# Half of a modulation's columns summed on VectorE, and parts of x / rms made behind the turned blocks

## The chip, the cores and the metric

One core of one Trainium2 chip runs the whole program in one launch. The metric is the device time of one execution in microseconds (us). The engines are named as the profile names them: PE is TensorE (PEld its weight loads), DVE is VectorE, ACT is ScalarE, POOL is GpSimd, SP is SyncE, whose queue carries the weight transfers.

## What is computed

Two transformer blocks on 256 tokens of width 1024, the second on the output of the first. What the change touches, in the reference's own words (batch 1; `c` is one row of 1024 values, `w_ada` 1024 x 6144):

```python
# first block
x = x + memory_cross_attention(x, mem, ...)          # 4 heads of 256, 256 memory tokens
x = x + swiglu(x, ffn_norm_g, w_gate, w_up, w_down)  # 1024 -> 2816 -> 1024
...
# second block
mod_lat = (silu(c) @ w_ada + b_ada)[:, None, :]
mod_ctx = silu(c_ctx) @ w_ada + b_ada
sh1, sc1, gt1, sh2, sc2, gt2 = split(mod_lat, 6)
h_lat = rms_norm(x, g_pre_mix) * (1 + sc1) + sh1
x = x + gt1 * rms_norm(token_mixer(h_lat, h_ctx, ...), g_post_mix)
h2 = rms_norm(x, g_pre_ffn) * (1 + sc2) + sh2
f = moe_ffn(h2, ...)        # 64 experts, 8 a token, and a shared one
x = x + gt2 * rms_norm(f, g_post_ffn)
```

Of `mod_ctx` only the first 2048 columns (`csh1`, `csc1`) are used.

## The kernel before, in words

The state `x` lies in SBUF as 128 partitions by 2 x 1024 (two tiles of 128 tokens). Dense products run in three passes of fp32r, the split of both operands into a high part and a rest: `mm3` (lines 643 to 645) issues hi x hi, lo x hi and hi x lo. A weight page is 128 x 2048 fp32, 1 MB. The class `Stream` plans all pages in one list; SP issues their transfers in that order (line 220) whenever the cap of the stage leaves room in a pool of 25 pages. A page that is to be split gets its high part `wh` from ScalarE (line 246) and its rest `wl` from VectorE (line 247), each in two halves of 128x1024. `CAP` holds the room and how many halves may be split ahead, per stage.

The program of each engine is static and in order. `weave(name, main, *sides)` sets the order around the change: `main` and `sides` are generators, `yield` ends a step, and the table `ORDER[name]` says behind which step of `main` each step of a side stands. The pieces are, in the order of the program:

- `ada(i)`, lines 934 to 958: 2048 columns of the modulation. Eight pages, four matmuls of 512 columns on each (line 941; the profile shows each as two records), with silu(c) and silu(c_ctx) as two of 32 columns of the stationary operand. Then a copy to SBUF (ACT, line 947), four transposes `adaT` (PE, line 950), and the sum with the bias into `mod` (DVE, line 953). `mod` holds 48 columns, one for each 128 values of the modulation.
- `cq` (weave at line 1062): `ada(0)`'s rest, the norm of the cross attention and its query product, with four steps of `ada(1)` behind it.
- `cross` (lines 1071 to 1127): scores `cl` (line 1078), row maximum `mx` (DVE, line 1081), exponential (ACT, line 1085), the division (DVE, line 1089), the transposes `ct` (PE, line 1100), their copies `PTc`, the product `co` (line 1116) and the product with w_co. The rest of `ada(1)` is woven in as its filler.
- `ffn` (weave at line 1165): `ffn_in` (lines 1139 to 1163) runs 11 units of 256 columns. A unit is two pages, w_gate and w_up, of 96 matmuls in all, silu of the gate (ACT, line 1159), the product with `w_up` (DVE, line 1160), and its split into `ah` (ACT, line 575) and `al` (DVE, line 576). Three steps of `ada(2)` are woven in. Then w_down, 11 pages.
- the mixer of the second block, and `post` (lines 1663 to 1680): x + gate x norm, the sum of squares, `newton` (1 / rms, a row of small DVE operations), `diag` (line 546: the diagonal matrices with which PE turns and scales x), and `xsh`, the high part of x / rms (ACT, line 1679). The other 20 matmuls of `ada(2)` stand in it, with their copy and transposes.
- `route()` (from line 1731): the turned blocks `tr` (PE, line 600), the modulation and split of each (ACT and DVE, lines 611 to 616), the logits `rt`, with the first half of the shared expert's products `s` among them, `xsl` (DVE, line 1747: the rest of x / rms beside `xsh`), the scores `sc` turned, and the selection of the experts from line 1758. The page for `xsl` comes free with the first page of the shared expert.
- the experts: 18 pages of them are planned ahead of the selection; the pages after those are asked for by the numbers (`eid`) that it gives.

## Time and profile before

| | us |
|---|---|
| three runs | 1213.98, 1216.49 (median), 1217.29 |
| the profiled execution | 1215.87 |
| its span | 1214.1 |
| PE busy in the span | 1161.0 (96%) |
| DVE busy | 632.8 (52%) |
| ACT busy | 466.0 (38%) |
| mean granted TensorE clock | 0.987 of full |

The span is what the profile covers, from the first to the last instruction; the time of the execution is a little longer. All times in the rows are counted from the span's start. A row of the timeline gives the start, the length, the engine, the line, the operation with the names of what it writes and reads, and in brackets how long the engine stood idle before it and which instruction ended that. Several equal instructions in a row are one row with their count. The granted clock is 1.00 at 2.4 GHz and 0.50 at 1.2 GHz; a window with a value between them holds some of both.

### The profile page before, as it was taken

Reading aid. Unit: us, or ns where it says so; the run is one execution under the profiler, and the core shown is the slowest. Engines: PE = TensorE matmul, PEld = TensorE weight load, DVE = VectorE, ACT = ScalarE, POOL = GpSimd, SP = SyncE. Lnnn points to the kernel's source line nnn. Section 1 sums busy time; section 2 is a strip of 40 time slices with the busy share of each in tenths; the row PEclk is TensorE's granted clock in tenths of the full one; section 3 lists DMA queues with packets and bytes.
Section 4 is the critical chain, followed back from the end, with each engine's and each line's share of the span. In section 5 each row is a group of like instructions: output and inputs, shape, how many; then the busy total and the mean of one; then the engine's idle time right before and its main releaser. Section 6 shows DMA issues by size and latency. Waiting matters only on the chain.

```text
span 1214.1 us, 18537 instructions
## 1 busy us (share of the span) xinstructions
PE 1161.0 (96%) x7391; PEld 832.7 (69%) x7391; DVE 632.8 (52%) x1280; ACT 466.0 (38%) x738; POOL 2.0 (0%) x9
## 2 busy tenths in 40 slices
PE   6999999999999999999999978999999999998986
PEld 6898869689999888998888757444444434442532
DVE  4688855565454457756784855343333223331323
ACT  4566246445344543875544542111111111110121
POOL 0000000000000000000000000000000000000000
PEclk9999999999999999999999988999999999999998
DMA  7934797644544654422546886999999999999994
GB/s 284 326 139 177 275 391 307 237 173 177 206 179 166 224 208 174 172 106 79 184 181 244 338 361 248 392 411 421 420 422 421 420 421 421 421 420 421 421 420 172
DMA packets 54096, 351.43 MB, mean 289 GB/s; under 512 B 6103, under 2 KB 8312, under 8 KB 12792
## 3 DMA queue, kind: packets, MB, share of 16 engines
q1 hardware_dynamic: 52080, 342.90, 71.7%
q10 hardware_dynamic: 1928, 7.33, 1.6%
q8 instruction: 59, 0.97, 0.3%
q14 instruction: 29, 0.24, 0.1%
HBM read 347.51 MB, written 2.69 MB: 288 GB/s over the span
## 4 chain that ended last, share of the span: by engine, by line
PE 79%; DMA 16%; DVE 2%; ACT 1%; issue 0%; SPq 0%; ACTq 0%; DVEq 0%
PE gu L1941 10%; DMA w<-in_w_expert_gu 8%; PE tsb L643 6%; PE tsb L645 6%; PE tsb L644 6%; PE ed L1970 6%; DMA w<-in_w_expert_down 5%; PE ga L1910 3%; PE acc L1980 3%; PE ws L643 3%; PE ws L645 3%; PE ws L644 3%; PE w_up L643 2%; PE w_gate L643 2%; PE w_gate L644 2%; PE w_up L645 2%
## 5 line engine op out<-in xcount | busy, mean ns | idle before, releaser
L247 DVE TENSOR_TENSOR wl<-w,wh 128x1024 fp32r<-128x1024 f32 (+1 forms) x210 | 242.2, 1200 | 79.1 <-ACT wh L246 68.9
L246 ACT ACTIVATE wh<-w 128x1024 fp32r<-128x1024 f32 (+1 forms) x210 | 204.9, 1039 | 48.4 <-DMA w<-in_w_in 14.1
L1941 PE MATMUL gu<-w,xe 128*32 128x512 f32 (+1 forms) x1216 | 204.9, 602 | 11.4 <-DMA w<-in_w_expert_gu 11.4
L1941 PEld LDWEIGHTS gu<-w,xe 128*32 128x32 f32 (+1 forms) x1216 | 60.9, 122 | 150.9 <-issue 118.2
L1970 PE MATMUL ed<-w,hT 128*32 128x512 f32 (+1 forms) x608 | 106.4, 597 | 3.0 <-DMA w<-in_w_expert_down 2.9
L643 PE MATMUL ws<-hi,wh 128*128 128x256 f32 x352 | 102.3, 291 | 4.6 <-ACT wh L575 2.5
L643 PE MATMUL tsb<-wh,hi 128*128 128x512 f32 x256 | 101.4, 396 | 1.6 <-ACT g1r L572 1.6
L645 PE MATMUL ws<-hi,wl 128*128 128x256 f32 x352 | 101.1, 287 | 0.8 <-DVE wl L247 0.8
L644 PE MATMUL ws<-lo,wh 128*128 128x256 f32 x352 | 100.9, 287 | 0.0
L645 PE MATMUL tsb<-wh,lo 128*128 128x512 f32 x256 | 99.8, 390 | 0.0
L644 PE MATMUL tsb<-wl,hi 128*128 128x512 f32 x256 | 99.8, 390 | 0.0
L1950 DVE TENSOR_TENSOR hh<-hh,gu 128x256 f32<-128x256 f32 x27 | 11.4, 421 | 151.0 <-ACT hh L1949 151.0
L1949 ACT ACTIVATE hh<-gu 128x256 f32<-128x256 f32 x27 | 10.4, 384 | 191.0 <-PE gu L1941 191.0
L580 ACT ACTIVATE ey<-ed,ws 128x512 fp32r<-128x512 f32 x54 | 37.1, 688 | 119.8 <-PE ed L1970 116.9
L581 DVE SCALAR_TENSOR_TENSOR ey<-ed,ws,ey 128x512 fp32r<-128x512 f32 x54 | 40.5, 751 | 75.1 <-ACT ey L580 72.9
L643 PEld LDWEIGHTS ws<-hi,wh 128*128 128x128 f32 x352 | 68.9, 196 | 7.4 <-ACT wh L575 3.9
L1970 PEld LDWEIGHTS ed<-w,hT 128*32 128x32 f32 (+1 forms) x608 | 28.8, 121 | 63.2 <-issue 49.1
L645 PEld LDWEIGHTS ws<-hi,wl 128*128 128x128 f32 x352 | 68.8, 195 | 1.2 <-DVE wl L247 1.0
L644 PEld LDWEIGHTS ws<-lo,wh 128*128 128x128 f32 x352 | 69.0, 196 | 0.2
L1980 PE MATMUL acc<-ey,gt 128*128 128x512 f32 x216 | 60.0, 411 | 0.0
L1980 PEld LDWEIGHTS acc<-ey,gt 128*128 128x128 f32 x216 | 37.5, 188 | 27.4 <-issue 21.4
L643 PEld LDWEIGHTS tsb<-wh,hi 128*128 128x128 f32 x256 | 48.1, 188 | 11.4 <-ACT g1r L572 2.1
(450 smaller groups left out, 2112.8 us busy)
## 6 DMA issues: line engine op xcount, KB each, us to landing
w<-in_w_expert_gu SPq DMA_DIRECT2D x128, 1024.0 KB, 19.8
w<-in_w_expert_down SPq DMA_DIRECT2D x60, 1024.0 KB, 19.7
w<-in_w_in SPq DMA_DIRECT2D x39, 1024.0 KB, 6.1
w<-in_w_ada SPq DMA_DIRECT2D x24, 1024.0 KB, 7.7
w<-in_w_gate SPq DMA_DIRECT2D x11, 1024.0 KB, 4.9
w<-in_w_up SPq DMA_DIRECT2D x11, 1024.0 KB, 6.7
w<-in_w_down SPq DMA_DIRECT2D x11, 1024.0 KB, 5.0
w<-in_w_out SPq DMA_DIRECT2D x8, 1024.0 KB, 5.3
```

The costliest lines, as they stand in the source:

```text
L246: kb.nc.scalar.activation(c.hi[:, s], c.raw[:, s], AF.Copy)
L247: kb.nc.vector.tensor_sub(c.lo[:, s], c.raw[:, s], c.hi[:, s].bitcast(F32))
L580: S.activation(hi, src, AF.Copy, scale=col)
L581: V.scalar_tensor_tensor(lo, src, col, hi.bitcast(F32), op0=OP.mult, op1=OP.subtract)
L643: PE.matmul(out, l[0], r[0], start=start, stop=False, skip_group_check=free)
L644: PE.matmul(out, l[0], r[1], start=False, stop=False, skip_group_check=free)
L645: PE.matmul(out, l[1], r[0], start=False, stop=stop, skip_group_check=free)
L1910: PE.matmul(b[:, i * w:i * w + w], xs[part][:, tt, dd * 128:dd * 128 + 128], oh_[:, tt, :], start=part + tt == 0, stop=part + tt == 2)
L1941: PE.matmul(b[w * e:w * e + w, :], xe[:, k, w * e:w * e + w], w3(gu[e][k // 4], a=4)[:, k % 4, :], start=k == 0, stop=k == 7, skip_group_c ...
L1950: V.tensor_mul(h, h, b[:, 256:512])
L1970: PE.matmul(b[w * e:w * e + w, :], hT_[:, f * 128 + w * e:f * 128 + w * e + w], w3(dn[e], a=2)[:, f, n * 512:n * 512 + 512], start=f == 0, ...
L1980: PE.matmul(sums[tt, n], gt[:, tt * 128:tt * 128 + 128], y[:, part * 1024 + n * 512:part * 1024 + n * 512 + 512], start=False, stop=stop a ...
```

## The change

The 6144 columns of `w_ada` are split in three. Columns 0 to 2047 stay `ada(0)`. Columns 2048 to 3071 go to `ada_half`: four pages, 32 matmuls of 256 columns, one copy of half the size, two transposes. It takes the place of `ada(1)`, and stands wholly in the cross part. Columns 3072 to 6143 go to `ada_rest`: their weights are laid out turned, so that a partition holds the 1024 weights of one column, and VectorE multiplies them by silu(c), a row that is the same on all partitions, and sums along the row into one column of `mod` (`accum_out`): 24 operations of 128x1024, two for each of 12 pages. The row is read by a broadcast transfer on ScalarE's queue (512 KB in SBUF) and goes through Silu on ScalarE. The pages are planned one behind each pair of w_gate and w_up and one behind the second page of w_down. `ada(2)` is gone, and with it its copy and its transposes. Total weight bytes are the same. The room of `ffn_in` goes from 10 to 9 pages, since the row takes one; by the planned order each turned page is asked for a unit ahead of its use.

The second part: `xsh` is made in `route()`, behind the logits and just ahead of `xsl`, in place of in `post`. By the built program both now wait for the first page of the shared expert to come free.

```diff
--- before.py
+++ after.py
     "cq": [
         [-1, -1, 3, 3, 5, 6],
         [1, 4, 6, 6, 7, 7, 10],
-        [1, 11, 12, 28],
     ],
...
     "ffn": [
         [-1, 0, 2, 2, 2, 2],
-        [12, 21, 21],
+        [6, 10, 14, 18, 22, 26, 30, 34, 38, 42, 46],
     ],
...
-       "cq1": (8, 5), "cross": (7, 3), "co": (10, 4), "ffn": (12, 3), "ffn_in": (10, 5), "z": (8, 5), "f0": (5, 4),
+       "cq1": (8, 5), "cross": (7, 3), "co": (10, 4), "ffn": (12, 3), "ffn_in": (9, 5), "z": (8, 5), "f0": (5, 4),
...
+    def plan_adaT(q):
+        plan(("adaT", q), "w_adaT_2", q, "raw")
...
-    plan_pair("w_cq", 0, 512, ada=(1, 0, 4))
-    plan_ada(1, 4)
+    plan_pair("w_cq", 0, 512)
+    for k in range(4):
+        plan(("adah", k), "w_adah_2", k, "raw")
...
-    for c0 in range(0, 2816, 256):
-        plan_cols("w_gate", c0, 256)
-        plan_cols("w_up", c0, 256)
-        if 0 < c0 // 256 <= 3:
-            plan_ada(2, c0 // 256 - 1, c0 // 256)
-    plan_cols("w_down", 0, 1024, 22)
+    for u in range(11):
+        plan_cols("w_gate", u * 256, 256)
+        plan_cols("w_up", u * 256, 256)
+        plan_adaT(u)
+    for u in range(11):
+        plan_cols("w_down", 0, 1024, 22, only=u)
+        if u == 1:
+            plan_adaT(11)
...
-    plan_ada(2, 3)
...
+    def ada_half():
+
+        b = bank("ada")
+        for k in range(8):
+            if k % 2 == 0:
+                c = st.get(("adah", k // 2))
+            for j in range(4):
+                PE.matmul(b[32 * j:32 * j + 32, 0:256], silw[:, k, :],
+                          c.raw[:, k % 2 * 1024 + j * 256:k % 2 * 1024 + j * 256 + 256],
+                          start=k == 0, stop=k == 7, skip_group_check=True, tile_position=(0, 32 * j))
+            if k % 2:
+                st.free(c)
+                if k < 7:
+                    yield
+        a = t2k("ada")
+        S.activation(a[:, 0:256], b[:, 0:256], AF.Copy)
+        b2 = bank("adaT")
+        for j in range(2):
+            PE.transpose(b2[:, j * 128:j * 128 + 128], a[:, j * 128:j * 128 + 128], ident)
...
+    def ada_rest():
+
+        t = page("crow")
+        crow, junk = t[:, 0:1024], t[:, 1024:2048]
+        nc.scalar.dma_start(crow, bass.AP(tensor=A["c_row"].tensor, offset=A["c_row"].offset, ap=[[0, 128], [1, 1024]]))
+        S.activation(crow, crow, AF.Silu)
+        for q in range(12):
+            c = st.get(("adaT", q))
+            for n in range(2):
+                V.scalar_tensor_tensor(junk, c.raw[:, n * 1024:n * 1024 + 1024], 1.0, crow, op0=OP.mult, op1=OP.mult,
+                                       accum_out=mod[:, 24 + 2 * q + n:25 + 2 * q + n])
+            st.free(c)
+            yield
+        V.tensor_add(mod[:, 24:48], mod[:, 24:48], cols[:, bada + 24:bada + 48])
+        rel(t)
+        yield
...
-    mods = [ada(i) for i in range(3)]
+    mods = [ada(0), ada_half(), ada_rest()]
...
-          turned_norm(xp, gcol("cross_norm_g")), ctx_prep(), itertools.islice(mods[1], 4))
+          turned_norm(xp, gcol("cross_norm_g")), ctx_prep())
...
-          itertools.islice(mods[2], 3))
+          itertools.islice(mods[2], 11))
...
+        if u == 1:
+            run_all(mods[2])
...
-        nh["hi"] = page("xsh", F32R)
-        for tt in range(2):
-            sl = slice(tt * 1024, tt * 1024 + 1024)
-            S.activation(nh["hi"][:, sl], xp[:, sl], AF.Copy, scale=nh["rs"][:, tt:tt + 1])
...
-    weave("post", chain(mods[2], act(after_ada2)), post())
+    weave("post", act(after_ada2), post())
...
-        nh["lo"] = page("xsl", F32R)
+        nh["hi"], nh["lo"] = page("xsh", F32R), page("xsl", F32R)
         for tt in range(2):
             sl = slice(tt * 1024, tt * 1024 + 1024)
+            S.activation(nh["hi"][:, sl], xp[:, sl], AF.Copy, scale=nh["rs"][:, tt:tt + 1])
             V.scalar_tensor_tensor(nh["lo"][:, sl], xp[:, sl], nh["rs"][:, tt:tt + 1], nh["hi"][:, sl].bitcast(F32),
                                    op0=OP.mult, op1=OP.subtract)
```

Where the rows of a static program stand now, at the three places of which the prediction speaks. First TensorE in the cross part, from the end of the query product to `co`; before:

```order
L941 MATMUL ada<-w,silw 32x512 x12
L1078 MATMUL cl<-kmT,qc 128x256 x16
L941 MATMUL ada<-w,silw 32x512 x8
L1100 MATMUL ct<-misc,quarters 128x128 x16
L941 MATMUL ada<-w,silw 32x512 x8
L950 MATMUL adaT<-misc,quarters 128x128 x4
L1116 MATMUL co<-PTc,vm 128x256 x8
```

and now:

```order
L1124 MATMUL cl<-kmT,qc 128x256 x16
L971 MATMUL ada<-w,silw 32x256 x16
L1146 MATMUL ct<-misc,quarters 128x128 x16
L971 MATMUL ada<-w,silw 32x256 x16
L982 MATMUL adaT<-misc,quarters 128x128 x2
L1162 MATMUL co<-PTc,vm 128x256 x8
```

The filler ahead of the scores is gone; the other two have twice as many matmuls of half the columns.

Second VectorE in the feed forward, the first two units (`quarters` is the unit's product, `crow,mod<-w,crow` a multiply-sum); before:

```order
L247 TENSOR_TENSOR wl<-w,wh 128x1024 x6
L1160 TENSOR_TENSOR quarters<-quarters,w_up 128x512
L576 TENSOR_TENSOR al<-quarters,ah 128x512
L247 TENSOR_TENSOR wl<-w,wh 128x1024 x3
L1160 TENSOR_TENSOR quarters<-quarters,w_up 128x512
```

and now:

```order
L246 TENSOR_TENSOR wl<-w,wh 128x1024 x3
L998 SCALAR_TENSOR_TENSOR crow,mod<-w,crow 128x1024 x2
L246 TENSOR_TENSOR wl<-w,wh 128x1024 x2
L1206 TENSOR_TENSOR quarters<-quarters,w_up 128x512
L580 TENSOR_TENSOR al<-quarters,ah 128x512
L246 TENSOR_TENSOR wl<-w,wh 128x1024 x4
L998 SCALAR_TENSOR_TENSOR crow,mod<-w,crow 128x1024 x2
L1206 TENSOR_TENSOR quarters<-quarters,w_up 128x512
```

Two multiply-sums stand between the splits and the product of each unit. On ScalarE, ahead of the first gate, stood six `wh` and the load of the table; now:

```order
L245 ACTIVATE wh<-w 128x1024 x3
L993 DMA crow<-in_c_row 128x1024
L994 ACT_TABLE_LOAD
L994 ACTIVATE crow<-crow 128x1024
L245 ACTIVATE wh<-w 128x1024 x2
L1205 ACTIVATE quarters<-w_gate 128x512
```

Two of the splits and the gate now stand behind the Silu that waits for the row.

Third ScalarE from `post` to the scores; before:

```order
L531 ACTIVATE sq,ss<-x 128x1024
L1679 ACTIVATE xsh<-x,ny 128x1024 x2
L947 ACTIVATE quarters<-ada 128x512
L612 ACTIVATE quarters<-tr,mod,mcol 128x256
...
L246 ACTIVATE wh<-w 128x1024
L1751 ACTIVATE quarters<-rt 64x256
```

and now:

```order
L535 ACTIVATE sq,ss<-x 128x1024
L616 ACTIVATE quarters<-tr,mod,mcol 128x256
...
L245 ACTIVATE wh<-w 128x1024
L1791 ACTIVATE xsh<-x,ny 128x1024 x2
L1796 ACTIVATE quarters<-rt 64x256
```

`xsh` has moved from ahead of the turned blocks' modulation to just ahead of the scores. On TensorE the 20 matmuls and 4 transposes between the last `ob` (the mixer's output) and `tr` are gone, and on VectorE the two small operations that make `mcol` stand ahead of the second newton.

## Rows read from the trace of the kernel before

**Rows 1.** The page, part 1: busy time of each engine.

```profile
PE 1161.0 (96%) x7391; PEld 832.7 (69%) x7391; DVE 632.8 (52%) x1280; ACT 466.0 (38%) x738; POOL 2.0 (0%) x9
```

**Rows 2.** Windows: length, busy time by engine, granted clock, DMA share, GB/s.

```profile
300.00:400.00 100.00, 100.00 (x835) 98.43 (x834) 51.55 (x52) 42.12 (x51) 0.00 (x0) 1.00 0.47 169
...
776.00:1180.00 404.00, 390.27 (x2386) 175.01 (x2382) 134.89 (x399) 73.06 (x125) 0.00 (x0) 1.00 1.01 420
```

**Rows 3.** Timeline, 210 to 232 us: start, length, engine, line, names, idle before.

```profile
210.40 2.78 PE L941 MATMUL ada<-w,silw 128*32 128x512 f32 x24
...
212.08 2.36 DVE L247 TENSOR_TENSOR wl<-w,wh 128x1024 fp32r<-128x1024 f32 x2 [2.61 <-ACT wh L246]
...
215.14 0.69 DVE L1081 TENSOR_REDUCE mx<-cl 128x2 f32<-128x512 f32 x1 [0.70 <-PE cl L1078]
...
225.14 0.63 PE L1100 MATMUL ct<-misc,quarters 128*128 128x128 f32 x4 [1.54 <-DVE quarters L1089]
...
225.70 1.92 PE L941 MATMUL ada<-w,silw 128*32 128x512 f32 x16
...
228.83 3.40 PE L1116 MATMUL co<-PTc,vm 128*128 128x256 f32 x15
```

**Rows 4.** Windows of one and two us in the cross part and behind `post`.

```profile
224.00:225.00 1.00, 0.00 (x0) 0.00 (x0) 0.52 (x3) 1.00 (x4) 0.00 (x0) 1.00 0.98 401
...
722.00:724.00 2.00, 2.00 (x18) 2.00 (x17) 1.31 (x3) 1.46 (x4) 0.00 (x0) 0.84 0.98 410
...
740.00:742.00 2.00, 0.40 (x7) 0.26 (x7) 1.26 (x2) 0.63 (x1) 0.00 (x0) 1.00 0.93 291
742.00:744.00 2.00, 0.79 (x4) 0.26 (x4) 1.79 (x11) 0.00 (x0) 0.00 (x0) 0.78 1.03 434
...
748.00:750.00 2.00, 2.00 (x7) 1.52 (x6) 0.46 (x3) 0.00 (x0) 0.00 (x0) 0.51 0.96 352
```

**Rows 5.** Timeline of VectorE in the feed forward, 295 to 334 us.

```profile
295.34 0.69 DVE L1160 TENSOR_TENSOR quarters<-quarters,w_up 128x512 f32<-128x512 f32 x1 [5.68 <-PE w_up L645]
296.73 0.69 DVE L576 TENSOR_TENSOR al<-quarters,ah 128x512 fp32r<-128x512 f32 x1 [0.70 <-ACT ah L575]
297.68 4.63 DVE L247 TENSOR_TENSOR wl<-w,wh 128x1024 fp32r<-128x1024 f32 x4 [0.26 <-ACT wh L246]
308.04 0.69 DVE L1160 TENSOR_TENSOR quarters<-quarters,w_up 128x512 f32<-128x512 f32 x1 [5.74 <-PE w_up L645]
...
319.56 0.69 DVE L1160 TENSOR_TENSOR quarters<-quarters,w_up 128x512 f32<-128x512 f32 x1 [4.55 <-PE w_up L645]
...
333.12 0.69 DVE L1160 TENSOR_TENSOR quarters<-quarters,w_up 128x512 f32<-128x512 f32 x1 [5.45 <-PE w_up L645]
```

**Rows 6.** Line 533, the sum of squares (min/median/max in ns).

```profile
L533 DVE SCALAR_TENSOR_TENSOR hi<-x x3: 1218/1225/1225, 177.4 to 471.4; 128x1024 fp32r<-128x1024 f32 x3
L533 DVE DVE_READ_ACCUMULATOR hi<-x x3: 82/83/83, 178.5 to 472.5; 128x1 f32 x3
```

**Rows 7.** DMA issues by line: KB each, median us to landing.

```profile
glf<-in_c_gl ACTq DMA_DIRECT2D x1, 896.0 KB, 7.6
```

**Rows 8.** Timeline of `post` and of the routing's start, 709 to 736 us.

```profile
709.56 2.48 DVE L1670 SCALAR_TENSOR_TENSOR x<-sq,ny,x 128x1024 f32<-128x1024 f32 x2
...
715.40 2.19 ACT L1679 ACTIVATE xsh<-x,ny 128x1024 fp32r<-128x1024 f32 x2 [3.37 <-DVE ny L523]
715.40 0.42 DVE L546 TENSOR_TENSOR quarters<-misc,ny 128x256 f32<-128x256 f32 x1
...
718.12 1.11 PE L950 MATMUL adaT<-misc,quarters 128*128 128x128 f32 x4 [7.72 <-ACT quarters L947]
...
719.03 5.47 PE L600 MATMUL tr<-quarters,x 128*128 128x128 f32 x32
...
732.55 2.48 DVE L1747 SCALAR_TENSOR_TENSOR xsl<-x,ny,xsh 128x1024 fp32r<-128x1024 f32 x2 [0.80 <-PE s L645]
...
735.48 0.29 DVE L1758 TENSOR_TENSOR quarters<-sc,brow 128x128 f32<-128x128 f32 x1 [0.45 <-PE sc L1755]
```

More of the change, by code (lines that the diff above doesn't have):

```diff
@@ L958, in ada @@
         yield
+    def ada_half():
[16 more added lines that the diff above has]
+            PE.transpose(b2[:, j * 128:j * 128 + 128], a[:, j * 128:j * 128 + 128], ident)
+        t2k_back(a)
+        V.tensor_add(mod[:, 16:24].rearrange("p (g b) -> p g b", g=4),
+                     b2[:, 0:256].rearrange("p (b g r) -> p g b r", b=2, g=4)[:, :, :, 0],
+                     cols[:, bada + 16:bada + 24].rearrange("p (g b) -> p g b", g=4))
+        yield
[13 more added lines that the diff above has]
+        rel(t)
+        yield
     mcol = cp.tile([128, 64], F32, name="mcol")
@@ L2221, in arrays @@
     out = {}
+    w = np.asarray(inputs["w_ada_2"]).reshape(1024, 6144)
+    inputs = {**inputs, "w_ada_2": w[:, 0:2048]}
     for name in _INS:
@@ L2224, in arrays @@
         out[name] = packed(a, _PACK[name]) if name in _PACK else np.ascontiguousarray(a)
+    out["w_adah_2"] = packed(w[:, 2048:3072], 1024)
+    out["w_adaT_2"] = w[:, 3072:].T.reshape(12, 2, 128, 1024).transpose(0, 2, 1, 3).reshape(12, 128, 2048)
+    out["c_row"] = out["c_2"].reshape(1024)
     out["cols"] = np.concatenate([out.pop(name).reshape(n, 128).T for name, n in VECTORS], 1)
```

## The prediction, made before the changed kernel ran

> **What bounds the kernel.** I read the page first. TensorE is busy 96% of the span [rows 1], so what matters is whether an instruction lies on TensorE's own path. The windows sharpen that: from 300 to 400 us TensorE is busy 100 of 100 us, with VectorE busy 51.55 and the DMA engines 0.47 of their capacity. From 776 to 1180 us the DMA share is 1.01, at 420 GB/s [rows 2]: there the expert weights set the pace. The change touches only what lies ahead of the experts. What it gains there reaches the end one for one, since the expert pages that depend on the routing can't be asked for before it is done.
>
> Then I read, in order of time, the four places from which the modulation's matmuls go. In the cross attention TensorE waits for the softmax [rows 3]. In the feed forward only TensorE is late: the VectorE product that ends each unit waits 4.55 to 5.74 us for w_up [rows 5]. In `post` nothing is dense: the chain is newton, diag, turned blocks, logits [rows 8]. The last view is the granted clock [rows 4].
>
> **The cq part** loses 4 of a burst of 36 matmuls. Twelve such matmuls (24 records) took 2.78 us [rows 3], 0.23 each, so −0.9 us.
>
> **The cross part.** The 12 matmuls just priced stood ahead of the scores, which can now start up to 2.78 us sooner. Then VectorE is late: the first maximum stands behind the split pair that ends at 212.08 + 2.36 = 214.44, and it ran at 215.14 [rows 3]. So the softmax gains 0.7 us and no more. Of the two fillers that remain, each has 16 matmuls of 256 columns in place of 8 of 512. At a price that goes with the columns, that is the same 1.92 us; at the full price of a 512-column one, it is 1.9 us more each. I take the first, since the other fp32 matmuls go by their columns: `co` with 256 takes 3.40/15 = 0.227 [rows 3], the turned blocks with 128, most of them at the lower clock, 5.47/32 = 0.171 [rows 8]. The copy and the transposes behind the second filler halve: of the 3.13 us between 225.70 and 228.83, the filler is 1.92, the rest 1.2, and I take off 0.3. Own gain −1.0 us, bounds −1.3 and +0.9.
>
> **The clock in the cross part** is the disputed term. TensorE now runs out of work between the shorter first filler and the last softmax: the scores move by up to 2.78 us, the softmax's end by 0.7, and only two sets of four transposes lie in the 4 to 5 us between. Before, it stood for 1.54 us [rows 3], and the clock held at 1.00 (2.4 GHz) through a microsecond with no matmul at all [rows 4]. What came at 740 to 743 is nearer to the new case: TensorE was busy 0.40 of 2 us, and the clock, 0.78 in the mean from 742, fell to half (1.2 GHz) at about 743.1 [rows 4]. It came back at 750. In `post`, TensorE resumed at 718.12 and the mean of 0.84 in 722 to 724 puts the rise at 722.64, 4.5 us later [rows 4, 8]. So a fall costs 4.5/2 = 2.25 us where the rise comes as in `post`, (750 − 743.1)/2 = 3.4 us where it comes as behind the routing, and nothing where the clock holds. I take a fall at 2.25, since the matmuls that follow are as dense as those of `post`.
>
> The Trainium skill (TensorE: Matmul & The Clock Gate, Part 4: PE-mode transpose) says that transposes don't count as busy for the clock; by it the fall would be all but sure and the sum below the right one. No row here separates the two, and the weight of the fall below rests on the rows at 740.
>
> **The feed forward** loses 12 matmuls on the bound engine. Its units are 11.52 us apart (308.04 to 319.56); with 4 modulation matmuls one took 12.70 (295.34 to 308.04), with 8 another 13.56 (319.56 to 333.12) [rows 5]. So 1.18 + 2.04 = 3.2 us go. VectorE gains two multiply-sums a unit (scalar_tensor_tensor, the product of a weight row and silu(c), summed along the row). The nearest row is the sum of squares, 128x1024 fp32 with an accumulator, 1.225 us [rows 6]; with its 0.08 readout 1.31, so 2.62 a unit. A unit's VectorE work now is four wl at 1.16 (4.63) and two operations of 0.69 [rows 5]: 6.0; 8.6 of 11.52 then. The added work hides in the wait for w_up; if it didn't, all 24 would cost 31 us. The weight pages add 11 transfers of 1 MB where three were; at a share of 0.47 [rows 2] there is room, and each is asked for a unit ahead of its use. The broadcast of c stands on ScalarE's queue ahead of Silu, two splits and the gate: its nearest row is the 896 KB transfer on that queue, 7.6 us [rows 7]. It is 512 KB; the gate has slack since the first pages are split ahead. Between 0 and +4 us, I take 0.
>
> **In `post`** the 20 matmuls cost nothing: TensorE stood idle for the 7.72 us up to 718.12 all the same [rows 8]. Removed with them are a ScalarE copy behind two xsh and four transposes. The turned blocks, at 719.03, can start when the diag ends, 715.40 + 0.42, plus 0.3 for two small VectorE operations now ahead of newton: 716.2, or −2.8 us. They meet a clock that is at half, as before; TensorE will have idled 10 us instead of 7.7. Before, 3.6 of their 5.47 us lay ahead of the rise at 722.64 [rows 4, 8]; if all of them do, they take another 1.7 us. I take 0.7: −2.1, bounds −2.9 and −1.1.
>
> Given back: xsh (2.19 us for two) now stands between the release by the shared expert's matmuls (732.55) and xsl (2.48 for two), where xsl alone stood [rows 8]. First xsh 1.10, two xsl 2.48: 736.13 in place of 735.03, and the selection that waited for TensorE until 735.48 waits for VectorE: +0.65 us. Were xsh free there, 0. Net −1.5 us, bounds −2.9 and −0.4.
>
> **The sum:** −0.9 − 1.0 + 2.25 − 3.2 + 0 − 1.5 = −4.4 us. The profiled execution took 1215.87 us (span 1214.1 and 1.8 around it), which gives 1211.5; the median of the three runs lies 0.6 above it, so I forecast **1212.1 us**. What a measurement can tell from no change is about 0.3%, 3.65 us: faster is under 1212.8, slower over 1220.1.
>
> **Rivals.**
> - *The clock holds in the cross part.* For it: a whole idle microsecond did nothing at 224. Against it: the gap is three times as long. The sum without 2.25 is −6.6: 1209.9 us.
> - *The gains are given back*: the clock stays at half as long as behind the routing (3.4), the turned blocks run wholly at half (1.7 in place of 0.7, so that `post` gives −0.5), and the broadcast costs 1.0 us. Then −0.9 − 1.0 + 3.4 − 3.2 + 1.0 − 0.5 = −1.2: 1215.3 us, no difference to be measured. Also here: the filler at full price.
> - *VectorE becomes the bound of the feed forward.* It is in order: multiply-sums stand ahead of the product, the product ahead of ScalarE's ah, and al (which waited 0.70) ahead of the next wl (0.26). Forced time per unit is 4.63 + 1.38 + 0.96 = 6.97 [rows 5] and two multiply-sums; it decides where one of these, with its wait for the page, takes over (11.52 − 6.97)/2 = 2.28 us. The sum of squares reads the same tensor twice, the new operation two tensors; but two different fp32 tensors took 2.48 for two without a sum [rows 8], which speaks against it. At twice the row, 2.53 with the readout, and a page half a microsecond late in each unit, a unit takes 6.97 + 5.06 + 0.5 = 12.53: 11 × 1.01 = 11.1 us, less the 3.2 that went: −0.9 − 1.0 + 2.25 + 7.9 − 1.5 = +6.8, 1223.3 us. The Trainium skill (Vector Engine (DVE) Microarchitecture Reference, 7. Points that are easy to get wrong) says that just this operation with two non-bf16 sources halves throughput, with no port left for the accumulator's readback; alone, without late pages, that is 1.2 us above before. Rows 6 disagree for one tensor read twice, and no row shows two.
> - *The change doesn't do what it says*: a page comes late and the multiply-sums hold back wl all the same. That lies between the last two.
>
> **Chances.** Forecast 0.42, clock holds 0.27, given back 0.22, VectorE 0.09. The forecast's own spread, 1210.5 to 1214, lies two thirds under 1212.8: faster is 0.28 of the forecast, 0.26 of the clock that holds and 0.02 of the gains given back, 0.56; slower is VectorE's 0.09 and 0.01 of the gains given back, 0.10; the rest, 0.34, is no difference. The low end is the clock that holds with `post` at its best, 1208.5; the high end takes in the given-back case and half of the step to VectorE's, 1218.0.
>
> **What would show it.** In the profile after: multiply-sums of 1.2 to 1.3 us, units of 11.52 us throughout with a VectorE wait for w_up of 2 us or more (wrong: VectorE never idle ahead of the product). In the cross part a clock under 1.00 between 222 and 230 us, or 1.00 throughout; `co` about a microsecond earlier if it holds, later if not. In `post` the turned blocks 3 us after newton's end minus its copy, xsh just ahead of xsl, and the selection waiting for VectorE. The expert stage should last as long as before; if it gets longer, the one-for-one passage is wrong.

## The result, and the profile after

| | before | after |
|---|---|---|
| median of five runs | 1216.49 us | 1208.74 us |
| lowest to highest | 1213.98 to 1217.43 | 1207.36 to 1210.34 |
| ratio of the runs | | 0.9935, 95% interval 0.992 to 0.9949 |
| span of the profiled execution | 1214.1 us | 1205.6 us |

The change makes the kernel faster: by 7.75 us between the medians, 6.2 to 9.7 by the interval. The forecast was 4.4. The page of after, part 1, which answers to [rows 1]:

```profile
PE 1150.4 (95%) x7321; PEld 833.4 (69%) x7321; DVE 661.1 (55%) x1328; ACT 466.3 (39%) x738; POOL 2.0 (0%) x9
```

TensorE's busy time falls by 10.6 us and VectorE's rises by 28.3, and the kernel follows TensorE. Where the time went is read best by stages, each from the start of one named instruction to the start of the next, in the profile of before, in a second profile of it (the run before_again below) and in that of after:

| stage, from ... to ... (us) | before | before again | after |
|---|---|---|---|
| start to the residual sum ahead of cq | 173.80 | 174.25 | 172.66 |
| cq: to the last pair of copies of its product (`qc`) | 35.99 | 35.99 | 35.14 |
| cross: to the first copy of `co` (`oh`) | 20.97 | 20.97 | 21.09 |
| to the first product of the feed forward | 53.06 | 53.04 | 53.07 |
| ten units, to the last product | 118.41 | 118.41 | 115.20 |
| w_down and the mixer, to the first newton of `post` | 305.16 | 305.26 | 305.12 |
| `post`, turned blocks, logits, to the selection | 28.09 | 28.22 | 25.73 |
| selection, to the expert numbers (`eid`) | 7.89 | 7.88 | 7.61 |
| to the first expert's product (`hh`) | 21.47 | 21.77 | 21.57 |
| experts, to the last norm | 443.39 | 442.37 | 442.58 |

The rows of cq, the units and `post` hold the gain: 0.85, 3.21 and 2.4 us, and 0.3 behind the selection. The cross part gives nothing. The start and the experts lie within what two profiles of the same kernel differ by (0.45 and 1.0 us), or the eleven later runs with the change do: 172.86 to 174.96 us for the start, 442.35 to 442.74 for the experts. So the 8.5 us between the two spans hold 1.1 of a start that happened to be short and some 0.8 of experts that happened to be long in the first profile of before. Without the start, the rows of before and after differ by 7.3 us, and those of the second profile of before and after by 6.8.

**The cross part.** The timeline of after, 219 to 227 us, which answers to [rows 3]:

```profile
219.85 0.63 PE L1146 MATMUL ct<-misc,quarters 128*128 128x128 f32 x4 [1.58 <-DVE quarters L1135]
...
222.36 0.63 PE L1146 MATMUL ct<-misc,quarters 128*128 128x128 f32 x4 [1.88 <-DVE quarters L1135]
...
222.91 2.99 PE L971 MATMUL ada<-w,silw 128*32 128x256 f32 x32
...
226.87 3.71 PE L1162 MATMUL co<-PTc,vm 128*128 128x256 f32 x16
```

and its windows (busy time of PE, PEld, DVE, ACT and POOL, then the granted clock, DMA share and GB/s), which answer to [rows 4]:

```profile
218.00:220.00 2.00, 0.42 (x5) 0.21 (x3) 0.88 (x5) 1.02 (x4) 0.00 (x0) 1.00 0.99 414
220.00:222.00 2.00, 0.48 (x4) 0.24 (x3) 0.88 (x3) 1.40 (x5) 0.00 (x0) 1.00 1.04 438
222.00:224.00 2.00, 1.64 (x24) 1.04 (x28) 1.87 (x4) 1.54 (x3) 0.00 (x0) 0.91 0.94 397
...
226.00:228.00 2.00, 1.61 (x7) 1.51 (x8) 0.17 (x1) 0.33 (x1) 0.00 (x0) 0.74 0.00 0
```

TensorE runs out of work at 218.3 and is busy for 0.42 us of the 2 us from 218 and for 0.48 of the 2 us from 220. The clock falls: a mean of 0.91 in 222 to 224 is half from 223.64 on, 0.74 in 226 to 228 is full again from 227.04 on. The filler behind the softmax, 1.92 us before, takes 2.99.

**The feed forward.** One unit on VectorE, which answers to [rows 5], and the multiply-sum's own line with its smallest, median and largest time in ns, which answers to [rows 6]:

```profile
341.89 4.63 DVE L246 TENSOR_TENSOR wl<-w,wh 128x1024 fp32r<-128x1024 f32 x4 [0.26 <-ACT wh L245]
346.44 1.22 DVE L998 SCALAR_TENSOR_TENSOR crow<-w,crow 128x1024 f32<-128x1024 f32 x1
347.59 0.08 DVE L998 DVE_READ_ACCUMULATOR crow<-w,crow 128x1 f32 x1
...
351.08 0.69 DVE L1206 TENSOR_TENSOR quarters<-quarters,w_up 128x512 f32<-128x512 f32 x1 [2.14 <-PE w_up L649]
...
362.60 0.69 DVE L1206 TENSOR_TENSOR quarters<-quarters,w_up 128x512 f32<-128x512 f32 x1 [2.14 <-PE w_up L649]
```

```profile
L998 DVE SCALAR_TENSOR_TENSOR crow<-w,crow x24: 1214/1224/1226, 276.2 to 414.1; 128x1024 f32<-128x1024 f32 x24
```

The sums take 1.224 us each and 0.08 for the readout, 2.5 us for the pair, in front of a product that waits 2.14 us for w_up all the same. So it is in eight of the eleven units; the first product waits 0.97 us, the last two 1.12 and 0.39. The eleven products are 11.52 us apart.

**Behind `post`.** The first newton of `post`, taken from the small VectorE addition that opens it, in before and in after:

```profile
707.39 0.15 DVE L1665 TENSOR_TENSOR ss<-ssq 128x2 f32<-128x2 f32 x1
```

```profile
702.28 0.15 DVE L1713 TENSOR_TENSOR ss<-ssq 128x2 f32<-128x2 f32 x1
```

TensorE, ScalarE and VectorE of after, in this order, and two windows for the clock; these answer to [rows 8]:

```profile
710.75 5.92 PE L604 MATMUL tr<-quarters,x 128*128 128x128 f32 x32 [9.90 <-DVE quarters L550]
```

```profile
724.42 2.19 ACT L1791 ACTIVATE xsh<-x,ny 128x1024 fp32r<-128x1024 f32 x2 [1.91 <-PE s L648]
```

```profile
725.61 2.48 DVE L1792 SCALAR_TENSOR_TENSOR xsl<-x,ny,xsh 128x1024 fp32r<-128x1024 f32 x2 [1.84 <-ACT xsh L1791]
728.01 0.29 DVE L1803 TENSOR_TENSOR quarters<-sc,brow 128x128 f32<-128x128 f32 x1
...
735.62 0.21 DVE L1856 CAST eid<-ord 1x76 int32<-1x76 f32 x1
```

```profile
704.00:706.00 2.00, 0.00 (x0) 0.00 (x0) 1.90 (x5) 0.24 (x1) 0.00 (x0) 0.73 1.03 434
...
714.00:716.00 2.00, 2.00 (x15) 2.00 (x15) 1.31 (x3) 1.46 (x4) 0.00 (x0) 0.71 0.00 0
```

The turned blocks start 8.47 us after the first newton; before it was 11.64. The clock fell at 704.9 and rose at 715.2. The two xsh now stand between the release by `s` (724.42) and xsl, and the selection (the row `quarters<-sc,brow`) starts when VectorE is through with xsl. From the first newton to that release it is 25.16 us in before (707.39 to 732.55) and 22.14 in after.

### The profile page after: what moved, and what is told of

It reads as the page before. It is cut to its first block, busy times and chain, and to the rows that moved or that the text cites. A ratio compares the mean times of both kernels' runs of the same rounds, so it can differ in the third digit from the quotient of the medians.

```text
span 1205.6 us, 18438 instructions
## 1 busy us (share of the span) xinstructions
PE 1150.4 (95%) x7321; PEld 833.4 (69%) x7321; DVE 661.1 (55%) x1328; ACT 466.3 (39%) x738; POOL 2.0 (0%) x9
## 4 chain that ended last, share of the span: by engine, by line
PE 68%; DMA 24%; DVE 4%; ACT 2%; issue 1%; SPq 0%; ACTq 0%; DVEq 0%
DMA w<-in_w_expert_gu 16%; PE gu L1986 7%; PE tsb L647 6%; PE tsb L648 6%; PE tsb L649 6%; DMA w<-in_w_expert_down 5%; PE ed L2015 4%; PE ws L649 3%; PE ws L647 3%; PE ws L648 3%; PE acc L2025 2%; PE ga L1955 2%; PE w_up L648 2%; PE w_up L647 2%; PE w_gate L649 2%; PE w_gate L648 2%
## 5 line engine op out<-in xcount | busy, mean ns | idle before, releaser
L649 PEld LDWEIGHTS tsb<-wh,lo 128*128 128x128 f32 x256 | 48.0, 188 | 10.2
```

What stands on the lines that cost most here:

```text
L649: PE.matmul(out, l[1], r[0], start=False, stop=stop, skip_group_check=free)
```

## The experiments

The runs stand in the order of the questions. "After" is the changed kernel; all edits are made to it, unless said otherwise. What is compared is mostly one stage of the table above, since a stage repeats within some 0.1 us where neither the clock nor the stream moves (that of w_down and the mixer moves by 1.1 us between the runs), and the time of the kernel within a few us.

### Is the cross part's small gain the clock? (ada1_back, ct_matmul, ct_turn)

The first run takes the cq and cross part of the change back:

```diff
-    plan_pair("w_cq", 0, 512)
-    for k in range(4):
-        plan(("adah", k), "w_adah_2", k, "raw")
+    plan_pair("w_cq", 0, 512, ada=(1, 0, 4))
+    plan_ada(1, 4)
...
-        for q in range(12):
+        for q in range(8):
...
-    mods = [ada(0), ada_half(), ada_rest()]
+    mods = [ada(0), ada(1), ada_rest()]
```

> Only the feed forward's and post's part of the change: columns 2048 to 4095 are multiplied on TensorE by ada(1) as before (eight pages, four matmuls of 512 columns on each, in cq and cross), columns 4096 to 6143 on VectorE from eight turned pages, xsh as in the changed kernel. Theory (of the time gained, the cq and cross part made only 0.7 us, since a clock that fell there took back what the missing filler gave): 0.7 us slower than the changed kernel, about 1209.4 us, with the clock at 1.00 in the cross part and the units of the feed forward at 11.52 us. Rival (the cq and cross part is worth the 1.9 us that its matmuls cost): 1.9 us slower, about 1210.6 us.

Median 1209.17 us (ratio to before 0.9946, interval 0.9929 to 0.9963), 0.4 above after. Its cq stage is 35.99 us and its cross stage 20.97, to the hundredth those of before; all later stages are those of after (units 115.20, `post` to the selection 25.63). So the four pages of turned columns and the smaller matmuls of the cross part are worth 0.73 us. That is the theory's number; the rival's 1.9 is out. Six later profiles have the cross part of after unedited, and their cross stage is 21.09 to 21.44 us, with a fall of the clock between 223.7 and 226.1; by them the two are worth 0.38 to 0.73.

The other two fill TensorE's gaps ahead of the last two sets of transposes with idle work:

```diff
                 b = bank("ct")
+                for _ in range(11 if tt else 0):
+                    PE.matmul(b[:, 0:128], ident, ident, start=True, stop=True)
                 for h2 in range(2):
```

(ct_turn has `PE.transpose(b[:, 0:128], ident, ident)` in the loop.)

> The changed kernel with 11 idle matmuls (128x128 on the identity, into the bank that the transposes then overwrite) ahead of each of the last two sets of four transposes in the cross attention, where TensorE stood idle for 1.6 and 1.9 us. Theory (the clock fell at 223.6 because TensorE had run out of work from 218.3 on): the granted clock stays at 1.00 from 220 to 230 us, the filler behind the softmax takes 1.9 us instead of 2.99, co starts 1.0 to 1.1 us earlier, and the kernel is 1.0 to 1.7 us faster than the changed kernel, 1207 to 1208 us. Rival (the fall costs nothing, as what follows waits for the splits of w_co): the clock holds, but the product with w_co starts when it did, within 0.3 us.

Median 1208.32 us (0.9939, 0.9922 to 0.9955), the same as after within the interval. The clock stayed at 1.00 in every window from 206 to 234 us, but the cross stage is 20.83 us, 0.26 less than after's, where 1.0 to 1.1 was expected. The idle work was too long, which the timeline of TensorE shows:

```profile
218.75 2.62 PE L1145 MATMUL ct<-misc 128*128 128x128 f32 x22
```

An fp32 matmul is two records in the trace; the 11 took 2.62 us, not the 1.3 that I had reckoned by the record, and pushed the real transposes back. The run with transposes does the same in half the time:

> As ct_matmul, but the 11 idle operations are transposes of the identity in place of matmuls with it: the same tiles, the same stretch. If transposes count for the clock as matmuls do, the clock stays at 1.00 from 220 to 230 us as there. If they don't, it falls to half at about 223.6 us as in the changed kernel, the filler takes about 3 us, and nothing is gained.

```profile
219.46 1.36 PE L1145 MATMUL ct<-misc 128*128 128x128 f32 x11
...
221.65 1.36 PE L1145 MATMUL ct<-misc 128*128 128x128 f32 x11
223.62 0.70 PE L1148 MATMUL ct<-misc,quarters 128*128 128x128 f32 x4 [0.60 <-DVE quarters L1135]
224.25 1.93 PE L971 MATMUL ada<-w,silw 128*32 128x256 f32 x32
```

```profile
220.00:222.00 2.00, 1.71 (x16) 1.42 (x15) 1.38 (x4) 0.52 (x4) 0.00 (x0) 1.00 1.01 422
222.00:224.00 2.00, 1.40 (x13) 1.10 (x12) 0.83 (x4) 2.00 (x6) 0.00 (x0) 1.00 1.02 430
```

One run, 1206.62 us. The clock stays at 1.00; the filler behind the softmax takes 1.93 us; the cross stage is 19.74 us, 1.35 less than after's. So the fall cost 1.35 us (up to 1.70 against the six other profiles), and without it the cross part of the change is worth 1.23 (20.97 to 19.74). And transposes alone, in stretches of 1.36 us, were enough to keep the clock up. This is one profile, but no other speaks against it: the clock held in the cross part in the three profiles with the old filler (before, before_again, ada1_back) and in the four with idle work in the gaps (ct_matmul, ct_turn and the two filled ones below), and fell in all seven without either.

### Does VectorE become the bound? (double_sums)

```diff
-            for n in range(2):
+            for n in (0, 0, 1, 1):
                 V.scalar_tensor_tensor(junk, ...
```

> The changed kernel with every multiply-sum on VectorE issued twice (48 in place of 24), so that VectorE's forced time in a unit of the feed forward is 6.97 + 4 x 1.31 = 12.2 us. Theory (VectorE has room up to 2.28 us per multiply-sum and is the bound beyond): units go from 11.52 to about 12.2 us, so 11 x 0.7 = 7 to 8 us longer than the changed kernel, about 1216 us, and TensorE waits for wl in each unit. Rival (the splits run far enough ahead, and the wait for ah overlaps with multiply-sums): units stay at 11.52 to 11.8 us, under 3 us longer.

One run, 1210.82 us, 2.1 above after's median. VectorE of one unit, and the only wait of TensorE that the view of waits has from 290 to 420 us:

```profile
308.13 0.68 DVE L1206 TENSOR_TENSOR quarters<-quarters,w_up 128x512 f32<-128x512 f32 x1
309.52 0.69 DVE L580 TENSOR_TENSOR al<-quarters,ah 128x512 fp32r<-128x512 f32 x1 [0.70 <-ACT ah L579]
310.47 4.63 DVE L246 TENSOR_TENSOR wl<-w,wh 128x1024 fp32r<-128x1024 f32 x4 [0.26 <-ACT wh L245]
315.01 1.22 DVE L998 SCALAR_TENSOR_TENSOR crow<-w,crow 128x1024 f32<-128x1024 f32 x1
...
319.96 0.68 DVE L1206 TENSOR_TENSOR quarters<-quarters,w_up 128x512 f32<-128x512 f32 x1
```

```profile
PE dn L647 <- DVE quarters L1206: 1.6, 1, 1.6
```

The unit is 11.83 us (308.13 to 319.96), and VectorE waits for nothing but ah (0.70) and wh (0.26): it is the bound. So the threshold stands, between two sums a unit, with 2.14 us to spare, and four. The price does not. The forced time comes to 11.83 and not 12.2, since operations in a row overlap a little (four sums and readouts take 4.94 us, not 5.24). And the 3.05 us by which VectorE fell behind over ten units did not hold TensorE, which has no other wait in that stretch. It paid once, 1.6 us, when the first use of the last units' product came. Half of the theory, then: the bound was right, and so was the sign, but of 7 to 8 us came 1.4 to 2.5 (the units with the stages on either side of them, against after and against the ten other profiles of the changed kernel and its variants), as the rival's under 3 has it.

### What does the clock cost in `post`? (busy_post, turns_post, turns84)

```diff
     def post():
+        dm = bank("dm")
+        for _ in range(76):
+            PE.matmul(dm[:, 0:128], ident, ident, start=True, stop=True)
         ss = small("ss", 2)
```

(turns_post has 64 and turns84 84 `PE.transpose(dm[:, 0:128], ident, ident)` in the loop.)

> The changed kernel with 76 idle matmuls (128x128 on the identity, into a bank of their own) between the mixer's last product and the turned blocks, where TensorE stood idle for 9.9 us and the clock fell at 704.9. At 0.115 each they take 8.7 us and end before the diag does. Theory (what the clock costs in post is the part of the turned blocks at half): the clock stays at 1.00, the 16 turned blocks take 3.7 us in place of 5.5, and the selection comes 1.7 to 2.2 us earlier; the kernel 1.5 to 2.2 us faster than the changed one, 1206.5 to 1207.5 us. Rival (the modulation of the blocks on VectorE and ScalarE sets the pace): under 0.7 us earlier.

Median 1212.72 us (0.9972, 0.996 to 0.9985), slower than after. The same wrong price: the 76 matmuls took 17.13 us and held up the turned blocks, which then ran in 3.74 us:

```profile
702.67 17.13 PE L1714 MATMUL dm<-misc 128*128 128x128 f32 x152
719.64 3.74 PE L604 MATMUL tr<-quarters,x 128*128 128x128 f32 x32
```

From the blocks' start to the selection it is 15.5 us here, 17.3 in after: 1.7 us for the clock, as the theory had it, but the run as a whole does not show that it can be had.

> As busy_post, but with idle operations that end in time: 64 transposes of the identity, 0.124 us each by ct_turn, 7.9 us in a stretch in which TensorE stood idle for 9.9. Theory (the clock costs post what lies at half of the turned blocks, and transposes hold it up): the clock stays at 1.00, the turned blocks take 3.7 us from about the same start, the selection comes 1.7 us earlier, the kernel 1.5 to 2.0 us faster than the changed one, 1206.8 to 1207.3 us. Rivals: the clock falls all the same (transposes alone don't hold it over 8 us): no gain; or the modulation behind the turned blocks sets the pace: under 0.7 us.

Median 1208.7 us (0.9941, 0.9925 to 0.9956), no gain in the time, and 0.4 in the stage to the selection (25.30 us). The 64 transposes took 7.15 us, 0.112 each, ended at 707.49 and left 2.97 us of idleness; the windows:

```profile
710.00:712.00 2.00, 1.54 (x13) 1.57 (x14) 0.73 (x2) 0.00 (x0) 0.00 (x0) 0.96 1.01 414
712.00:714.00 2.00, 2.00 (x11) 2.00 (x11) 1.16 (x3) 1.60 (x3) 0.00 (x0) 0.50 0.06 21
```

The clock fell 0.16 us ahead of 712, in the blocks' second microsecond. Neither rival was tested by this: the work had ended too early.

> As turns_post, with 84 idle transposes in place of 64. The 64 took 7.15 us (0.112 each) and left TensorE idle for 2.97 us ahead of the turned blocks, and the clock fell at 711.9 all the same. 84 take 9.4 us of the 9.9 to 10.1 us. Theory (as in turns_post): the clock stays at 1.00, the turned blocks take 3.7 us in place of 5.6 to 6.6, the shared expert's first page is released 1.7 to 2.2 us earlier against post's first newton (20.0 to 20.4 us in place of 22.05), and the kernel is 1.5 to 2.0 us faster than the changed one, 1206.8 to 1207.3 us. Rival (the modulation behind the blocks sets the pace): released no more than 0.7 us earlier.

```profile
702.48 9.33 PE L1714 MATMUL dm<-misc 128*128 128x128 f32 x84
...
712.58 3.81 PE L604 MATMUL tr<-quarters,x 128*128 128x128 f32 x32 [0.78 <-issue]
```

```profile
704.00:708.00 4.00, 4.00 (x39) 4.00 (x38) 3.62 (x14) 0.46 (x1) 0.00 (x0) 1.00 0.98 387
708.00:712.00 4.00, 3.81 (x35) 3.57 (x33) 3.65 (x15) 0.69 (x2) 0.00 (x0) 1.00 0.78 289
712.00:716.00 4.00, 3.42 (x30) 3.45 (x31) 1.95 (x5) 1.64 (x3) 0.00 (x0) 1.00 0.55 227
```

Median 1206.03 us (0.9911, 0.9895 to 0.9928), 2.7 below after. The clock holds through 9.33 us in which TensorE did nothing but transposes, the blocks take 3.81 us in place of 5.92, and the stage to the selection is 24.12 us, 1.6 less than after's. From the first newton to the release of the shared expert's first page it is 20.54 us where after has 22.14. The theory's 20.0 to 20.4 was 0.1 too low; the rival is out. The rest of the 2.7 lies in other stages, above all in the 20.35 us to the first expert in place of 21.57. The edit does not touch that stage, but the clock behind the selection was at half for 3.4 us in this profile (737.24 to 740.66) and for 6.8 in after (735.64 to 742.48), for a reason that stays open:

```profile
736.00:738.00 2.00, 1.53 (x9) 1.09 (x10) 1.43 (x7) 0.38 (x1) 0.00 (x0) 0.81 1.03 434
...
740.00:742.00 2.00, 2.00 (x9) 1.63 (x8) 0.24 (x2) 0.00 (x0) 0.00 (x0) 0.83 1.01 406
```

So of the 2.7 the edit's own part is 1.6.

### What did the move of xsh cost? (xsh_in_post, filled_xsh)

```diff
         nh["dg"], nh["dq"] = diag(nh["rs"])
+        nh["hi"] = page("xsh", F32R)
+        for tt in range(2):
+            sl = slice(tt * 1024, tt * 1024 + 1024)
+            S.activation(nh["hi"][:, sl], xp[:, sl], AF.Copy, scale=nh["rs"][:, tt:tt + 1])
         yield
...
-        nh["hi"], nh["lo"] = page("xsh", F32R), page("xsl", F32R)
+        nh["lo"] = page("xsl", F32R)
...
-            S.activation(nh["hi"][:, sl], xp[:, sl], AF.Copy, scale=nh["rs"][:, tt:tt + 1])
```

> The changed kernel with xsh made in post again, as before the change. Theory (the move puts xsh on the path to the selection and costs 0.65 us; ScalarE is idle in post): the selection comes 0.6 to 0.7 us earlier against the end of the shared expert's first page, and the kernel is 0.5 to 0.7 us faster, about 1208.1 us. Rival (the page that xsh holds from post on keeps a weight page out, and the blocks' modulation queues behind xsh on ScalarE): the turned blocks' modulation or an expert's transfer comes later, and the kernel is as fast or slower.

Median 1209.02 us (0.994, 0.9926 to 0.9954): not to be told from after. The selection comes 2.93 us behind the release, as before, and 3.59 in after: 0.66, as the sum had it. But from the release to the expert numbers it is 10.82 us in before and here, 11.20 in after: 0.38. A later selection found the shared expert's matmuls, which stand ahead of the ranks on TensorE, already done, so 0.28 came back. In this run the clock rose late in the blocks (6.50 us for them, 5.92 in after), which took the gain. The same edit without that noise, on the kernel filled below:

> As filled, with xsh made in post again. In xsh_in_post the clock rose later in the turned blocks than in the changed kernel, which hid the price of the move; here the clock is at 1.00 throughout, so that nothing else differs. Theory (the move costs what the selection waits for xsh, less what the shared expert's matmuls in front of the ranks had to wait for anyway): from the release of the shared expert's first page to the expert numbers 10.8 us in place of 11.2, and from post's first newton to the numbers 31.3 to 31.4 in place of 31.7; in the time of the kernel no difference that can be told, 1203 to 1204 us. Rival (ScalarE's xsh holds up the blocks' modulation now that the blocks come sooner): 31.7 us or more from newton to the numbers.

From the release to the numbers 10.83 us in place of 11.18; from the first newton to the numbers 31.49 in place of 31.73. So the move costs 0.24 to 0.38 us on the path. The expectation's 31.3 to 31.4 was a little too good, since ScalarE's xsh ends at 711.06 and the first block's modulation on ScalarE stands behind it until 711.14; the rival holds in that much. Median 1202.24 us (0.9883, 0.9867 to 0.99).

The clock was not at 1.00 throughout, as the expectation had it. It fell at 734.7, behind the numbers (732.36), so that the two stretches compared are clear of it, and it fell in spite of the 15 transposes of the routing that the next experiment brings:

```profile
734.00:736.00 2.00, 2.00 (x9) 1.63 (x9) 1.50 (x8) 0.38 (x1) 0.00 (x0) 0.68 1.01 426
736.00:738.00 2.00, 2.00 (x6) 1.57 (x5) 0.53 (x4) 0.00 (x0) 0.00 (x0) 0.50 1.01 414
```

From the numbers to the first expert it is 20.36 us here.

### Is there more of the same behind the selection? (turns_route)

The clock fell once more in after, as it did before, while VectorE worked on the ranks. Windows of after:

```profile
734.00:736.00 2.00, 0.53 (x4) 0.27 (x4) 1.82 (x10) 0.00 (x0) 0.00 (x0) 0.91 1.00 418
736.00:738.00 2.00, 1.53 (x7) 1.01 (x6) 0.96 (x6) 0.38 (x1) 0.00 (x0) 0.50 1.01 426
```

```diff
         tb_ = bank("rT")
+        for _ in range(15):
+            PE.transpose(tb_[:, 256:384], ident, ident)
         PE.matmul(ob[0:1, 128:128 + NV], ...
```

> The changed kernel with 15 idle transposes of the identity (1.9 us) behind the ranks of the routing, where TensorE waits 2.3 us for VectorE. There the clock fell at 735.6, and the shared expert's second product and the first gathers ran at half until 742.2. Theory (what runs at half behind the selection is on the path to the first expert): the clock stays at 1.00, ten matmuls of the shared expert take 2.3 us in place of 4.3, the first expert's products start 2 to 3 us earlier, and the kernel is 1.5 to 3 us faster than the changed one, 1206 to 1207 us. Rival (the expert stage hangs on the stream of weights from the numbers on, which don't come earlier): within 0.5 us of the changed kernel.

```profile
734.88 1.83 PE L1853 MATMUL rT<-misc 128*128 128x128 f32 x15
...
737.35 0.29 PE L1854 MATMUL ord<-pv__6421,misc 64*1 64x76 f32 x2 [0.64 <-DVE pv__6421 L1846]
```

```profile
734.00:736.00 2.00, 1.50 (x18) 1.43 (x18) 1.27 (x5) 0.63 (x1) 0.00 (x0) 1.00 0.74 209
736.00:738.00 2.00, 1.12 (x10) 0.67 (x9) 1.82 (x10) 0.00 (x0) 0.00 (x0) 1.00 0.96 406
```

Median 1207.26 us (0.9927, 0.9912 to 0.9942), 1.5 below after; the intervals overlap, and the stage decides: from the expert numbers to the first expert's product 18.94 us in place of 21.57, 2.6 less, with the experts' stage at 442.50 as ever. So what is won ahead of the experts reaches the end. But the 15 transposes do not hold the clock in every run: it held in this profile and in that of filled, and fell in that of filled_xsh, where the stage took 20.36 us. What decides between them is open.

### All three places filled (filled)

The 84 transposes in `post`, the 15 in the routing, and in the cross part:

```diff
-        [-1, -1, -1, -1, 1, 1, 3, 3, 5, 6],
+        [-1, -1, -1, -1, 1, 2, 3, 3, 5, 6],
...
                 b = bank("ct")
+                for _ in range((0, 0, 6, 11)[tt * 2 + hp]):
+                    PE.transpose(b[:, 0:128], ident, ident)
                 for h2 in range(2):
```

The first line puts a page of the second filler between the two pairs of sets of transposes.

> The changed kernel with TensorE kept busy at its three sparse places: in the cross part a quarter of the filler moved between the last sets of transposes, and 6 and 11 idle transposes ahead of them; in post the 84 of turns84; in the routing the 15 of turns_route. Theory (the three are apart in time and what each saves reaches the end): 1.3 to 1.9 in the cross part (from query product to co's copy 19.2 to 19.7 us in place of 21.1), 1.7 to 2.0 in post, 2.6 in the routing (from the numbers to the first expert 18.9 us), 5.6 to 6.5 in all: 1202.2 to 1203.1 us. Rival (the expert stage hangs on its stream, or the longer filler holds the transposes up): 1205 us or more.

Median 1203.69 us (0.9899, 0.988 to 0.9918; four runs from 1201.47 to 1206.54). The cross stage is 18.87 us, 2.2 under after's, and below the 19.2 to 19.7 expected; `post` to the selection 24.13, 1.6 less; to the first expert 18.95, 2.6 less: 6.4 in all by the stages, 5.05 between the medians, half a us short of what was expected. TensorE in the cross part:

```profile
219.25 1.07 PE L971 MATMUL ada<-w,silw 128*32 128x256 f32 x16
...
221.40 1.36 PE L1145 MATMUL ct<-misc 128*128 128x128 f32 x11
223.30 0.70 PE L1148 MATMUL ct<-misc,quarters 128*128 128x128 f32 x4 [0.54 <-DVE quarters L1135]
```

With filled_xsh this is the fastest kernel of the study; the two cannot be told apart by their intervals. Both lie below before and, with intervals that end at 0.9918 and 0.99, just below after's 0.992 to 0.9949.

### The kernel before again (before_again)

No edit.

> The kernel before once more, for a second profile of it. The stages that the change doesn't touch are compared: from the start to the first block's first residual sum 173.8 us in the first profile of before, 172.7 to 174.5 in those of kernels with the change; from the first dynamic expert's product to the end 443.4 us against 442.4 to 442.7. If both differences are chance from run to run, this profile lies in the others' ranges in both; if the expert stage got shorter by the change, it has 443.4 again.

1215.84 us in its one run; the stages stand in the first table. The experts took 442.37 us, so that the 443.39 of the first profile was chance. The start, 174.25 us, lies in the others' range, and the 172.66 of after's profile below all of them.

## Why the prediction was right, and where its sizes were off

The time was inside the range by 0.24 us, on its low side; the direction, and faster by more than 0.3%, were the likeliest case. That the median is inside and not just outside is in part luck: two of the five runs lie under the range's low end of 1208.5. Term by term:

| term of the sum | forecast | by the stages |
|---|---|---|
| cq, four matmuls | −0.9 | −0.85 |
| cross, without the clock | −1.0 | −1.23 (before against ct_turn) |
| the clock in the cross part | +2.25 | +1.35 (after against ct_turn) |
| feed forward, twelve matmuls | −3.2 | −3.21 |
| broadcast of c | 0 | +0.01 (53.06 to 53.07) |
| turned blocks earlier, clock included | −2.1 | −3.0 (25.16 to 22.14) |
| xsh and xsl on the path | +0.65 | +0.38 |
| sum | −4.4 | −6.6 |

**Right** were cq and, to the hundredth, the units. These were the surest step: the price was taken from units with and without the matmuls, not from the matmuls' own records, and the work that took their place lay in a wait that the rows showed. The mechanism in the cross part was right too: the clock fell, at 223.64, behind the gap that was foreseen, and with the gap filled it held. So was the passage to the end: the experts took 442.35 to 442.74 us whatever came ahead of them. No run puts the matmuls of the feed forward or of `post` back by themselves; for these two the gain rests on the stages of before and after alone.

**Two sizes were off.** The step "I take a fall at 2.25" took the 4.5 us of `post` as the time at half; it was 3.4 us here (223.64 to 227.04), and of the half of it, 1.7, 1.35 reached the stage (1.35 to 1.70 by the seven profiles with such a fall). In `post` the blocks started 3.17 us earlier and not 2.8: the two small VectorE operations that I priced at 0.3 went into a gap, and newton starts 0.11 us behind the readout in both profiles. The 0.7 for a longer time at half was a term that chance decides: in seven profiles of kernels with the change and nothing added on TensorE at this place the blocks take 5.57 to 6.59 us (after's 5.92 is in the middle), in the two of before 5.47 and 5.79. The blocks of after took 0.45 us longer than before's, and only 0.15 of it reached the release: 3.17 less 0.15 is the 3.0 of the table. The prediction's bound for blocks wholly at half is a little low as well: by its own figures 5.47 − 3.6 = 1.9 us of them lay behind the rise, not 1.7.

The rest, from 6.6 to the 7.75 of the medians, is no more than what the medians scatter by (the interval ends at 6.2).

Of the rivals, **the clock holds** gave the time nearest to the measured one, 1209.9 us, but not by its mechanism. **The gains given back** would have needed a fall as long as that behind the routing. **VectorE as the bound** is refuted by the row of 1.224 us: two different fp32 tensors with an accumulator take what one tensor read twice took [rows 6], and no more than two different ones without a sum, 2.48 for two [rows 8]. By these rows the Trainium skill (Vector Engine (DVE) Microarchitecture Reference, 7. Points that are easy to get wrong), which has such a sum at half the throughput, isn't borne out here. Four sums a unit cost VectorE what two would have cost at twice the row, and the loss was 1.4 to 2.5 us; the step of that rival that failed is that a unit's delay passes to TensorE at once.

The other rule, that transposes don't count as busy for the clock (the Trainium skill, TensorE: Matmul & The Clock Gate, Part 4: PE-mode transpose), is contradicted as well where a clock at 1.00 has to be held: in turns84 it stayed there through 9.33 us of transposes alone. Whether transposes alone raise it from half, no run here shows. The fall in the cross part came because TensorE was idle, not because what it did were transposes: with more transposes in the same gaps it did not come.

## What to carry to other kernels

Price work that is taken off the bound engine by comparing stretches with and without it, and look whether what remains leaves that engine sparse: here a filler had held the clock up, and the fall that came without it took back all that its removal gave. Where an engine must wait anyway, idle transposes that end just ahead of the awaited operand bought 1.4 to 2.6 us at each of three places, though at one of them not in every run. Reckon the length of such a stretch from a run: one that was too long here was paid in full, and one that ended 3 us early bought 0.4. An in-order engine that fell behind a little in each unit was paid for here where its last result was first used, not in each unit.

## What the runs showed of the hardware that was not expected

- Transposes of fp32 128x128 on the identity ran at 0.112 to 0.124 us each, and the granted clock held at 1.00 through 9.33 us of them (turns84), as through 17.13 us of matmuls (busy_post); the fp32 matmul of the same tiles is two records and took 0.23 us.
- The turned blocks, started behind the same idleness of TensorE, took 5.57 to 6.59 us from run to run, by when the clock rose among them, 3.7 to 5.8 us behind their start: an effect of some 1 us that no edit made.
- The same 15 transposes in the same wait held the clock in two profiles and not in a third.
- A multiply-sum over two fp32 tensors of 128x1024 in SBUF took 1.224 us, as one over a single tensor does, and in a row of them one started every 1.27 us, readout included.
